# Moving half rotations and crossing halves by DMA instead of by TensorE and copies, in a three-layer fp32 transformer kernel

## The chip, the cores and the metric

The kernel runs on one core of a Trainium2 chip. The metric is the device time of one execution in microseconds; the figure quoted is the median of three runs.

## The reference

A sequence of 512 tokens with 1024 channels goes through three layers, all in float32. The first layer mixes a windowed grouped-query attention (8 query heads, 2 key heads, 64 channels each, a band of 128 tokens each way, a learned sink in the softmax) with a multi-scale pooling; the second a latent attention with a gated linear recurrence; both are followed by an MLP with squared ReLU. The third mixes a gated short convolution, a sparse attention (compressed, selected and windowed keys; for 512 tokens the last two are causal over everything) and a dilated attention (three pairs of heads with distances 1, 4 and 16), followed by an embedding gate and a norm.

What the change touches in it is the rope of the first layer's queries and keys,

```
x1, x2 = xf[..., :half], xf[..., half:]
concatenate([x1 * cos - x2 * sin, x2 * cos + x1 * sin])      # half = 32
```

and the score products `q @ k.T` of the windowed, sparse and dilated heads, with the maximum of each row that the softmax subtracts.

## The kernel before

All activations lie channel-major: a block is a tile of 128 channels by 512 tokens. Weights come from DRAM in units of 128 by 1024. For accuracy each float32 operand is cut into a high part in the matmul's fast format (`hi`, made by a copy) and a remainder (`lo`, made by a subtraction on VectorE or GpSimd), and each product is three matmuls: hi by weight hi, hi by weight lo, lo by weight hi (`mm3`). So TensorE reads weight splits `wh`, `wl`, and VectorE makes `wl` for each unit. For the later layers the splits of weights are made ahead and kept in DRAM (`keep_ahead`, tiles `kr`, `khi`, `klo`, `wk`), and fetched when needed.

**The order of the work** is written out by a planner in the program itself. `_Flow` keeps a clock `fl.now` that advances with each matmul; `_Engine` keeps a time at which VectorE, ScalarE or GpSimd would be free, from a cost formula. Main work and fill work are generators; side chains (`go`) are resumed when their due time has come. Each resumption emits instructions, so the order in which instructions stand in every engine's queue follows from that clock. `tt` gives an elementwise operation to VectorE or GpSimd and `copy` gives a copy to ScalarE or GpSimd, whichever the clock expects to finish first; an operand in PSUM keeps it off GpSimd. Transfers are all issued from SP's queue, in the order of emission, and `wl["dma"]` is the clock's guess of when the transfers issued so far are through.

**The places that the change touches.**

`rope64` (lines 1268 to 1284) turns five blocks of the first layer (one of keys, four of queries). It copies the projected block from PSUM to `zs`, multiplies `zs` on TensorE with a 128 by 128 permutation (`C("perm")`) that swaps the 32-channel halves of each head, and forms `a = zs * cos + swapped * sin` with tables `cosr`, `sinr` that hold the norm's scale; the swapped block is read from PSUM.

```
        ps2 = yield from takec("tr")
        mm(ps2, C("perm"), zs, True, True, 0.86)
        ...
        V.tensor_mul(b_, ps2, sinr)
```

`q_stacks` (956 to 965) makes two query tiles from a block z with two heads of 64 channels: for one head the upper 64 rows hold the high part of z and the lower 64 its remainder, for the other the reverse. Writing a remainder to the other half of the rows is done by the subtraction itself, one for each head. It is called for ten blocks: four of the first layer, `nq0` to `nq2`, and `dq0` to `dq2`.

`k_stacks` (967 to 978) makes for each of the block's two heads a tile `kh` with the high part of that head's 64 rows in both halves, and a tile `kl` with its remainder in both halves. That takes four copies and four subtractions of 64 rows. It is called for six blocks: one of the first layer, `ks`, `kw`, and `dk0` to `dk2`. A score is then two matmuls, `kh` by q and `kl` by q.

`Head.expo` (1004 to 1022) takes for each query block of 128 tokens the maximum of its scores from PSUM (`reduce_max`); in the windowed heads, whose scores carry a scale, it then scales it and takes the minimum with the sink (`mx`, then `nm`). ScalarE then forms the exponentials `p` with their sums. Scores of several query blocks share a PSUM bank: in the windowed heads blocks 0 and 3 (256 keys each), block 1 and block 2 (384 keys each); in the causal heads blocks 0 and 2 (128 and 384); in two dilated heads blocks 0 and 1 (128 and 256) and blocks 2 and 3 (256 each).

The first layer's attention (`attend`, jobs `job0`) starts a head's scores when its query and key stacks are there and interleaves them with fill: the remaining query blocks, the pooling and the first half of the output product.

Of the kernel before, what the change touches and what calls it, by code (L numbers as in the profile page):

```python
# [11 lines left out]
F32R = mybir.dt.float32r  # L12
# [6 lines left out]
P = 128  # L19
# [17 lines left out]
for _k, _w in _PRM:  # L37
# [3 lines left out]


_CST = (
    ("ident", 128), ("perm", 128), ("icnt", 64), ("v_cmp", 4),
    ("cos64", 512), ("sin64", 512), ("tqe", 512), ("tqo", 512), ("tk", 512),
    ("m_lo", 384), ("m_cmp", 128), ("m_d4", 512), ("m_d16", 512),
)
NKEEP = 324
_CO = {}
_n = 0  # L50
for _k, _w in _CST:
# [189 lines left out]
def _constants():  # L241
    f32 = np.float32
    cst = np.zeros((P, NCST), f32)

    def put(name, a):
        o, n = _CO[name]
        cst[:, o:o + n] = np.asarray(a, f32).reshape(P, n)

    r = np.arange(P)
    put("ident", np.eye(P))  # L250
    perm = np.zeros((P, P), f32)
    src = (r // 64) * 64 + (r % 64 + 32) % 64
    perm[src, r] = 1.0
    put("perm", perm)
    t = np.arange(T, dtype=f32)

    def rope(half):
        inv = (10000.0 ** (-(np.arange(half, dtype=f32) / f32(half)).astype(np.float64))).astype(f32)
        ang = (t[:, None] * inv[None, :]).astype(f32).astype(np.float64)
        j = r % (2 * half)  # L260
        sgn = np.where(j < half, -1.0, 1.0)
        return np.cos(ang)[:, j % half].T, np.sin(ang)[:, j % half].T * sgn[:, None]

    cs, sn = rope(32)
    put("cos64", cs)
    put("sin64", sn)
    cs, sn = rope(16)
    one = np.ones((64, T))
    put("tqe", np.concatenate([one, cs[:32], sn[:32]]))
    put("tqo", np.concatenate([cs[:32], sn[:32], one]))  # L270
    put("tk", np.concatenate([cs[:64], sn[:64]]))
    ic = np.zeros((4, 2, 8))
    for g, wd in enumerate((2, 4, 8, 16)):
        tt = np.arange(T)
        cnt = np.clip(tt + wd // 2, 0, T) - np.clip(tt - wd // 2, 0, T)
        ic[g, 0] = 1.0 / cnt[:8]
        ic[g, 1] = 1.0 / cnt[-8:]
    put("icnt", np.broadcast_to(ic.reshape(1, 64), (P, 64)))
    a, c = r[:, None], r[None, :]
    lo, up = np.where(c <= a, 0.0, NEG), np.where(c >= a, 0.0, NEG)  # L280
    put("m_lo", np.concatenate([lo, up, lo], axis=1))
    for dl in (4, 16):
        res = (a - c) % dl == 0
        full = np.where(res, 0.0, NEG)
        diag = np.where(res & (c <= a), 0.0, NEG)
        put(f"m_d{dl}", np.concatenate([full, full, full, diag], axis=1))
    tq = (np.arange(NQ)[None, :] * P + r[:, None])[:, :, None]
    n = np.arange(32)[None, None, :]
    ok = (16 * n + 31 <= tq) & (n < 31)
    put("m_cmp", np.where(ok, 0.0, NEG))  # L290
    put("v_cmp", ok.any(-1))
    return cst
# [196 lines left out]
def tile_hybrid(ctx: ExitStack, tc: tile.TileContext, wt, xT, pT, prm_d, cst_d, out):  # L489
# [24 lines left out]
    def blk(name="b", dt=F32, n=T):  # L514
        return bp.tile([P, TB], dt, tag="b", bufs=NB, name=uid(name))[:, 0:n]

    def small(n, name="s", dt=F32):
        return sp.tile([P, n], dt, tag=f"s{n}", bufs=24, name=uid(name))
# [19 lines left out]
    def takec(tag):  # L538
        while (t := bank(tag)) is None:
            yield 0.1  # L540
        return t
# [10 lines left out]
    def waitc(*tasks):  # L552
        for t in tasks:
            while not t.done:
                yield 0.1

    def f(ap):
        return ap.bitcast(F32)

    def mm(o, l, r, start, stop, us):  # L560
        PE.matmul(o, l, r, start=start, stop=stop, skip_group_check=True)  # L561
        fl.now += us
# [18 lines left out]
    def copy(out, src, scale=None):  # L581

        n, ps = width(out), src.space == PSUM
        sc = 1.0 if scale is None else scale
        e = first((S, 0.06 + n / 1090.0), *(() if ps else ((G, 0.07 + n * 0.00117 + fl.gc),)))
        if e is S:
            S.activation(out, src, AF.Copy, scale=sc)
        else:
            G.tensor_scalar(out, src, sc, 1.0, op0=ALU.mult, op1=ALU.mult)
# [185 lines left out]
    def C(name, n=None):  # L775
        o = _CO[name][0]
        n = n or _CO[name][1]
        if o + n <= NKEEP:
            return cst[:, o:o + n]
        t = blk("cst")  # L780
        nc.sync.dma_start(t[:, :n], cst_d[:, o:o + n])
        return t
# [154 lines left out]
    def v_stack(z):  # L937
# [15 lines left out]
        yield  # L953
        return lambda kb, h: r[kb // 2][0][:, kb % 2, h, :, :]

    def q_stacks(z, dst, i):

        qs = [blk("q", F32R), blk("q", F32R)]
        for r0, q in zip((0, 64), qs):
            copy(q[r0:r0 + 64], z[r0:r0 + 64])  # L960
        yield
        for r0, q in zip((0, 64), qs):
            V.tensor_sub(q[64 - r0:128 - r0], z[r0:r0 + 64], f(q[r0:r0 + 64]))
        yield
        dst[i], dst[i + 1] = qs

    def k_stacks(z, dst, i=0):

        ks = [(blk("kh", F32R), blk("kl", F32R)) for _ in range(2)]
        for r0, (kh, kl) in zip((0, 64), ks):  # L970
            copy(kh[r0:r0 + 64], z[r0:r0 + 64])
            copy(kh[64 - r0:128 - r0], z[r0:r0 + 64])
        yield
        for r0, (kh, kl) in zip((0, 64), ks):
            V.tensor_sub(kl[r0:r0 + 64], z[r0:r0 + 64], f(kh[r0:r0 + 64]))
            V.tensor_sub(kl[64 - r0:128 - r0], z[r0:r0 + 64], f(kh[r0:r0 + 64]))
        yield
        dst[i], dst[i + 1] = ks


# [11 lines left out]
    class Head:  # L992
# [11 lines left out]
        def expo(self, qbs, ps):  # L1004

            sc = self.scale
            for qb, o in qbs:
                n = self.pr[qb].shape[1]
                c = self.nm[:, qb:qb + 1]
                if sc == 1.0:  # L1010
                    V.reduce_max(c, ps[:, o:o + n], axis=AX.X, negate=True)
                else:
                    mx = small(1, "mx")
                    V.reduce_max(mx, ps[:, o:o + n], axis=AX.X)
                    V.tensor_scalar(c, mx, -sc, self.nsink, op0=ALU.mult, op1=ALU.min)
            yield
            for qb, o in qbs:
                n = self.pr[qb].shape[1]
                S.activation(self.pr[qb], ps[:, o:o + n], AF.Exp, bias=self.nm[:, qb:qb + 1], scale=sc,
                             accum_out=self.den[:, qb:qb + 1])  # L1020
            give("sc")
            yield
# [245 lines left out]
    def rope64(ps, then):  # L1268

        zs = blk("zs")  # L1270
        S.activation(zs, ps, AF.Copy)
        give("mm")
        yield
        yield from waitc(rp)
        ps2 = yield from takec("tr")
        mm(ps2, C("perm"), zs, True, True, 0.86)
        a, b_ = blk("ra"), blk("rbb")
        tt(ALU.mult, a, zs, cosr)
        yield
        V.tensor_mul(b_, ps2, sinr)  # L1280
        give("tr")
        tt(ALU.add, a, a, b_)
        yield
        yield from then(a)
# [1129 lines left out]
```

## Time and profile before

| | |
|---|---|
| median of 3 runs | 1483.72 us (1482.23 to 1487.07) |
| profiled execution | 1487.06 us, its span 1485.3 us |
| TensorE, weight loads | 1455.1 us (98%), 1179.5 us (79%) |
| VectorE, ScalarE, GpSimd | 912.5, 639.1, 327.0 us |
| granted TensorE clock | 0.989 |
| data moved by DMA | 291 MB, 196 GB/s |

PE is TensorE, PEld its weight load, DVE VectorE, ACT ScalarE, POOL GpSimd and SP SyncE, which issues the transfers. Matmuls overlap, so TensorE's busy time is the time in which at least one is under way. Most instructions of VectorE, ScalarE and GpSimd stand at line 363, most matmuls at 561 and transposes at 565, since small helpers issue them; tiles tell them apart, by names without their numbers.

### The profile page before, as it was taken

Reading aid. Unit: us, or ns where it says so; the run is one execution under the profiler, and the core shown is the slowest. Engines: PE = TensorE matmul, PEld = TensorE weight load, DVE = VectorE, ACT = ScalarE, POOL = GpSimd, SP = SyncE. Lnnn points to the kernel's source line nnn. Section 1 sums busy time; section 2 is a strip of 40 time slices with the busy share of each in tenths; the row PEclk is TensorE's granted clock in tenths of the full one; section 3 lists DMA queues with packets and bytes.
Section 4 is the critical chain, followed back from the end, with each engine's and each line's share of the span. In section 5 each row is a group of like instructions: output and inputs, shape, how many; then the busy total and the mean of one; then the engine's idle time right before and its main releaser. Section 6 shows DMA issues by size and latency. Waiting matters only on the chain.

```text
span 1485.3 us, 18855 instructions
## 1 busy us (share of the span) xinstructions
PE 1455.1 (98%) x6783; PEld 1179.5 (79%) x6786; DVE 912.5 (61%) x1419; ACT 639.1 (43%) x1174; POOL 327.0 (22%) x295
## 2 busy tenths in 40 slices
PE   9999999999999999799999999999999999999998
PEld 6778878888888887688888888888887788888787
DVE  6996864656334458987775665757755566536513
ACT  5675432323222345477342433434521575324623
POOL 4541220302102026442120220202110000111242
PEclk9999999999999999899999999999999999999999
DMA  7112688898322453332599999999855322345352
GB/s 233 43 50 79 203 275 282 262 303 283 120 91 97 146 212 143 123 132 72 173 312 318 344 322 330 333 321 331 305 206 199 113 86 108 120 171 210 116 191 93
DMA packets 117741, 291.44 MB, mean 196 GB/s; under 512 B 13072, under 2 KB 13584, under 8 KB 117648
## 3 DMA queue, kind: packets, MB, share of 16 engines
q1 hardware_dynamic: 117648, 290.25, 57.5%
q8 instruction: 53, 0.87, 0.2%
q14 instruction: 40, 0.33, 0.1%
HBM read 205.26 MB, written 84.93 MB: 195 GB/s over the span
## 4 chain that ended last, share of the span: by engine, by line
PE 84%; DVE 8%; DMA 2%; issue 2%; ACT 2%; POOL 0%; SPq 0%; POOLq 0%; DVEq 0%; ACTq 0%
PE mm L561 74%; PE sc L561 4%; PE tr L565 3%; PE av L561 3%; DVE sg L363 2%; DMA kr<-in_wt_dram 1%; PE tr L561 1%; DVE lo L363 1%; DVE mx L363 1%; DVE q L363 1%; ACT p L363 1%; DVE nm L363 0%; DVE wl L363 0%; DMA pin<-in_pT_dram 0%; DMA wr<-in_wt_dram 0%
## 5 line engine op out<-in xcount | busy, mean ns | idle before, releaser
L561 PE MATMUL mm<-hi,wh 128*128 128x512 f32 (+1 forms) x1276 | 510.5, 400 | 2.4 <-ACT hi L363 1.7
L561 PE MATMUL mm<-hi,wl 128*128 128x512 f32 (+1 forms) x1276 | 502.0, 393 | 1.4 <-DVE wl L363 1.4
L561 PE MATMUL mm<-lo,wh 128*128 128x512 f32 (+1 forms) x1276 | 501.1, 393 | 0.1
L561 PEld LDWEIGHTS mm<-lo,wh 128*128 128x128 f32 x1276 | 241.6, 189 | 56.8 <-DVE lo L363 2.1
L561 PEld LDWEIGHTS mm<-hi,wh 128*128 128x128 f32 x1276 | 242.0, 190 | 54.6 <-ACT hi L363 3.3
L561 PEld LDWEIGHTS mm<-hi,wl 128*128 128x128 f32 x1276 | 241.8, 190 | 51.5 <-DVE wl L363 2.1
L363 ACT ACTIVATE khi<-kr 128x512 fp32r<-128x512 f32 x120 | 75.9, 632 | 315.0 <-DMA kr<-in_wt_dram 305.6
L561 PE MATMUL mm<-ul,wh 128*128 128x512 f32 x512 | 202.0, 394 | 1.6 <-DVE ul L363 1.6
L561 PE MATMUL mm<-uh,wl 128*128 128x512 f32 x512 | 202.6, 396 | 0.0
L561 PE MATMUL mm<-uh,wh 128*128 128x512 f32 x512 | 202.0, 395 | 0.5 <-ACT uh L363 0.5
L363 DVE TENSOR_TENSOR wl<-wr,wh 128x1024 fp32r<-128x1024 f32 (+1 forms) x144 | 179.0, 1244 | 10.8 <-ACT wh L363 10.0
L363 DVE TENSOR_TENSOR klo<-kr,khi 128x512 fp32r<-128x512 f32 x150 | 122.5, 818 | 100.0 <-ACT khi L363 89.4
L363 ACT ACTIVATE wh<-wr 128x1024 fp32r<-128x1024 f32 (+1 forms) x142 | 146.5, 1032 | 44.3 <-PE mm L561 34.4
L363 DVE TENSOR_TENSOR x<-x,mm 128x512 f32<-128x512 f32 x112 | 76.9, 686 | 133.2 <-PE mm L561 131.3
L363 POOL TENSOR_TENSOR ma<-ma 128x512 f32<-128x512 f32 x62 | 85.4, 1378 | 275.0 <-ACT uh L363 228.4
L561 PEld LDWEIGHTS mm<-ul,wh 128*128 128x128 f32 x512 | 96.6, 189 | 24.5 <-DVE ul L363 2.1
L561 PEld LDWEIGHTS mm<-uh,wh 128*128 128x128 f32 x512 | 96.5, 189 | 23.9 <-ACT uh L363 0.9
L561 PEld LDWEIGHTS mm<-uh,wl 128*128 128x128 f32 x512 | 96.4, 188 | 22.2
L363 ACT ACTIVATE p<-sc,nm 128x512 f32<-128x512 f32 (+3 forms) x136 | 75.3, 557 | 33.9 <-DVE nm L363 25.3
L363 POOL TENSOR_SCALAR khi<-kr 128x512 fp32r<-128x512 f32 x30 | 32.2, 1075 | 254.1 <-DMA kr<-in_wt_dram 178.7
L363 DVE TENSOR_TENSOR pl<-tr,ph 128x512 fp32r<-128x512 f32 (+2 forms) x108 | 66.1, 624 | 29.9 <-ACT ph L363 29.1
L363 DVE SCALAR_TENSOR_TENSOR ma<-mm,rb 128x512 f32<-128x512 f32 x64 | 44.1, 689 | 48.6 <-PE mm L561 48.1
(291 smaller groups left out, 1642.4 us busy)
## 6 DMA issues: line engine op xcount, KB each, us to landing
wr<-in_wt_dram SPq DMA_DIRECT2D x144, 512.0 KB, 5.3
kr<-in_wt_dram SPq DMA_DIRECT2D x150, 256.0 KB, 5.9
wk<-khi SPq DMA_DIRECT2D x150, 256.0 KB, 6.0
wk<-klo SPq DMA_DIRECT2D x150, 256.0 KB, 5.7
wh<-wk SPq DMA_DIRECT2D x74, 512.0 KB, 3.3
wl<-wk SPq DMA_DIRECT2D x74, 512.0 KB, 4.2
x<-xs SPq DMA_DIRECT2D x16, 256.0 KB, 5.1
x<-in_xT_dram SPq DMA_DIRECT2D x8, 256.0 KB, 5.4
```

Of the source, the lines that this page charges most:

```text
L363: return fn(*a, **k)
L561: PE.matmul(o, l, r, start=start, stop=stop, skip_group_check=True)
L565: PE.transpose(o, i, idn)
```

## The change

The permutation goes, with its table. `rope64` copies `zs` into a tile `zw` with four transfers of 32 rows each from SBUF to SBUF, issued from SP's queue, and multiplies `zw` by `sinr` on VectorE or GpSimd. `q_stacks` copies the whole block once for one head and its lower half for the other, takes one remainder of the whole block, and moves the two remainder halves to where they belong with two transfers of 64 rows. `k_stacks` makes each head's half once, by two copies and two subtractions, and fills the other half with four transfers. After them the planner waits for a guessed landing (`moved`). `expo` takes the maxima of one bank's query blocks with one reduction where they are equally wide, and scales them together.

```
 _CST = (
-    ("ident", 128), ("perm", 128), ("icnt", 64), ("v_cmp", 4),
+    ("ident", 128), ("icnt", 64), ("v_cmp", 4),
...
-NKEEP = 324
+NKEEP = 196
...
+    def move(dst, src):
+
+        nc.sync.dma_start(f(dst), f(src))
+        wl["dma"] = max(wl["dma"], fl.now) + 0.4
+
+    def moved():
+        return max(wl["dma"], fl.now) + 2.0 - fl.now
+
+    up, dn = slice(0, 64), slice(64, 128)
+
     def q_stacks(z, dst, i):
 
-        qs = [blk("q", F32R), blk("q", F32R)]
-        for r0, q in zip((0, 64), qs):
-            copy(q[r0:r0 + 64], z[r0:r0 + 64])
-        yield
-        for r0, q in zip((0, 64), qs):
-            V.tensor_sub(q[64 - r0:128 - r0], z[r0:r0 + 64], f(q[r0:r0 + 64]))
-        yield
-        dst[i], dst[i + 1] = qs
+        qa, qb, lo = blk("q", F32R), blk("q", F32R), blk("ql", F32R)
+        copy(qa, z)
+        copy(qb[dn], z[dn])
+        yield
+        V.tensor_sub(lo, z, f(qa))
+        yield
+        move(qb[up], lo[dn])
+        move(qa[dn], lo[up])
+        yield moved()
+        dst[i], dst[i + 1] = qa, qb
 
     def k_stacks(z, dst, i=0):
 
-        ks = [(blk("kh", F32R), blk("kl", F32R)) for _ in range(2)]
-        for r0, (kh, kl) in zip((0, 64), ks):
-            copy(kh[r0:r0 + 64], z[r0:r0 + 64])
-            copy(kh[64 - r0:128 - r0], z[r0:r0 + 64])
-        yield
-        for r0, (kh, kl) in zip((0, 64), ks):
-            V.tensor_sub(kl[r0:r0 + 64], z[r0:r0 + 64], f(kh[r0:r0 + 64]))
-            V.tensor_sub(kl[64 - r0:128 - r0], z[r0:r0 + 64], f(kh[r0:r0 + 64]))
-        yield
+        (ha, la), (hb, lb) = ks = [(blk("kh", F32R), blk("kl", F32R)) for _ in range(2)]
+        copy(ha, z)
+        copy(hb[dn], z[dn])
+        yield
+        V.tensor_sub(la, z, f(ha))
+        V.tensor_sub(lb[dn], z[dn], f(hb[dn]))
+        yield
+        move(hb[up], hb[dn])
+        move(ha[dn], ha[up])
+        move(lb[up], lb[dn])
+        move(la[dn], la[up])
+        yield moved()
         dst[i], dst[i + 1] = ks
...
         def expo(self, qbs, ps):
 
             sc = self.scale
-            for qb, o in qbs:
+            ns = [self.pr[qb].shape[1] for qb, _ in qbs]
+
+            sets = [qbs] if len(set(ns)) == 1 else [[q] for q in qbs]
+            for g in sets:
+                (qb, o), m = g[0], len(g)
                 n = self.pr[qb].shape[1]
-                c = self.nm[:, qb:qb + 1]
+                c = self.nm[:, qb:g[-1][0] + 1:max(1, g[-1][0] - qb)]
+                p3 = ps[:, o:o + m * n].rearrange("p (a n) -> p a n", n=n)
                 if sc == 1.0:
-                    V.reduce_max(c, ps[:, o:o + n], axis=AX.X, negate=True)
+                    V.reduce_max(c, p3, axis=AX.X, negate=True)
                 else:
-                    mx = small(1, "mx")
-                    V.reduce_max(mx, ps[:, o:o + n], axis=AX.X)
+                    mx = small(2, "mx")[:, :m]
+                    V.reduce_max(mx, p3, axis=AX.X)
                     V.tensor_scalar(c, mx, -sc, self.nsink, op0=ALU.mult, op1=ALU.min)
...
+        zw = blk("zw")
+        for r in range(0, P, 32):
+            move(zw[r:r + 32], zs[(r ^ 32):(r ^ 32) + 32])
+        t = fl.now + moved()
         yield from waitc(rp)
-        ps2 = yield from takec("tr")
-        mm(ps2, C("perm"), zs, True, True, 0.86)
         a, b_ = blk("ra"), blk("rbb")
         tt(ALU.mult, a, zs, cosr)
-        yield
-        V.tensor_mul(b_, ps2, sinr)
-        give("tr")
+        yield max(0.0, t - fl.now)
+        tt(ALU.mult, b_, zw, sinr)
         tt(ALU.add, a, a, b_)
```

## Rows read from the trace of the kernel before

**Rows 1.** The page: TensorE's busy time, and the chain that ended last by engine.

```profile
PE 1455.1 (98%) x6783; PEld 1179.5 (79%) x6786; DVE 912.5 (61%) x1419; ACT 639.1 (43%) x1174; POOL 327.0 (22%) x295
...
PE 84%; DVE 8%; DMA 2%; issue 2%; ACT 2%; POOL 0%; SPq 0%; POOLq 0%; DVEq 0%; ACTq 0%
```

**Rows 2.** Busy us of each engine (instructions) in single stretches, granted clock, DMA share, GB/s.

```profile
20.00:60.00 40.00, 40.00 (x181) 30.74 (x180) 33.07 (x44) 14.83 (x29) 26.37 (x20) 1.00 0.30 87
60.00:110.00 50.00, 44.73 (x244) 35.80 (x243) 47.24 (x111) 40.83 (x105) 19.17 (x19) 0.97 0.13 40
...
200.00:220.00 20.00, 17.90 (x70) 13.84 (x69) 12.02 (x15) 6.92 (x10) 4.56 (x4) 0.91 0.86 292
...
570.00:640.00 70.00, 59.64 (x251) 47.93 (x250) 62.62 (x86) 31.53 (x57) 40.54 (x31) 0.88 0.32 114
...
1100.00:1370.00 270.00, 270.00 (x1412) 218.32 (x1414) 150.22 (x315) 113.66 (x287) 24.12 (x32) 0.99 0.41 148
```

**Rows 3.** Waits of TensorE, 55 to 130 us: total, times, longest.

```profile
PE tr L565 <- ACT p L363: 2.4, 3, 1.4
PE mm L561 <- DVE wl L363: 1.4, 2, 0.8
```

**Rows 4.** Timeline of TensorE around the fourth rotation: start us, us, instruction.

```profile
44.93 0.39 PE L561 MATMUL mm<-lo,wh 128*128 128x512 f32 x1
...
45.16 1.02 PE L561 MATMUL tr<-zs,cst 128*128 128x512 f32 x2
...
45.61 0.79 PE L561 MATMUL mm<-hi,wh 128*128 128x512 f32 x1
...
46.25 0.40 PE L561 MATMUL mm<-hi,wl 128*128 128x512 f32 x1
...
46.71 0.40 PE L561 MATMUL sc<-kh,q 128*128 128x256 f32 x2
```

**Rows 5.** VectorE's groups by form, 20 to 130 us: busy us, mean ns, idle before.

```profile
L363 DVE TENSOR_TENSOR q<-ra,q 64x512 fp32r<-64x512 f32 x8 | 9.5, 1192 | 0.3
...
L363 DVE TENSOR_SCALAR nm<-mx,nsink 128x1 f32<-128x1 f32 x32 | 6.8, 214 | 1.1
...
L363 DVE TENSOR_REDUCE mx<-sc 128x1 f32<-128x256 f32 x16 | 6.6, 414 | 0.0
...
L363 DVE TENSOR_TENSOR kl<-ra,kh 64x512 fp32r<-64x512 f32 x4 | 4.4, 1112 | 0.0
...
L363 DVE TENSOR_TENSOR rbb<-tr,cst 128x512 f32<-128x512 f32 x5 | 3.4, 685 | 0.7 <-PE tr L561 0.7
```

**Rows 6.** Timeline of VectorE: a maximum over 512 columns.

```profile
1343.73 0.69 DVE L363 TENSOR_REDUCE nm<-sc 128x1 f32<-128x512 f32 x1 [1.39 <-PE sc L561]
```

**Rows 7.** Timeline of GpSimd and VectorE at 51 us.

```profile
51.10 2.14 POOL L363 TENSOR_TENSOR ra<-ra,rbb 128x512 f32<-128x512 f32 x1 [3.89 <-DVE rbb L363]
52.01 1.78 DVE L363 TENSOR_TENSOR ra<-zs,cst 128x512 f32<-128x512 f32 x1
```

**Rows 8.** The page's DMA issues: count, KB each, median us to landing.

```profile
wk<-khi SPq DMA_DIRECT2D x150, 256.0 KB, 6.0
...
xs<-x SPq DMA_DIRECT2D x8, 256.0 KB, 2.1
```

**Rows 9.** Timeline: the last remainders of two key stacks, and a score.

```profile
38.77 4.49 DVE L363 TENSOR_TENSOR kl<-ra,kh 64x512 fp32r<-64x512 f32 x4
...
1350.51 2.81 DVE L363 TENSOR_TENSOR kl<-z,kh 64x512 fp32r<-64x512 f32 x4 [0.76 <-ACT kh L363]
...
1356.44 0.40 PE L561 MATMUL sc<-kh,q 128*128 128x512 f32 x1
```

**Rows 10.** Waits in SP's queue, 15 to 130 us: total, times, longest.

```profile
SPq L622 <- DVE wl L363: 55.5, 8, 15.9
SPq L622 <- POOL wl L363: 47.3, 5, 21.9
```

**Rows 11.** Timeline of ScalarE at 206 us: idle before it, and what ended it.

```profile
206.74 0.63 ACT L363 ACTIVATE khi<-kr 128x512 fp32r<-128x512 f32 x1 [4.60 <-DMA kr<-in_wt_dram]
```

More of the change, by code (lines that the diff above doesn't have):

```diff
@@ L250, in _constants @@
     put("ident", np.eye(P))
[L251 to L254, printed above, removed]
     t = np.arange(T, dtype=f32)
```

## The prediction

> **What bounds the kernel now.** I read the page's busy table first, then its chain of work that ended last, then busy times of eleven stretches, then the waits of single ones. TensorE is busy 98% of the span and carries 84% of the chain [rows 1]. So a microsecond of matrix work removed is a microsecond won, unless the other engines can't follow. The stretches say where they can't. From 20 to 60 us TensorE is busy all 40 us. In the first attention, 60 to 110, it is busy 44.73 of 50 us while VectorE is busy 47.24: 5.3 us of idle time, and the granted clock of 0.97, partly the lower level of 1.2 GHz, costs 50 x 0.03 = 1.5 us more [rows 2]. Its waits there name the exponentials, which wait for maxima taken on VectorE, and weight remainders made on VectorE [rows 3]. In 200 to 220, at the start of the first MLP, are 2.1 us of idle time and 20 x 0.09 = 1.8 us of lost clock; in 570 to 640, behind the recurrent block, 10.4 us idle. From 1100 to 1370 TensorE is never idle [rows 2].
>
> The change touches three places: the rope and stacks at 20 to 60 us with the attention behind them, the stacks of the sparse attention (from 1105), and those of the dilated attention (to 1356).
>
> **The permutation matmuls.** Each rope loses one fp32 matmul, which runs as two passes. Around the fourth, the first pass starts at 45.16, one ordinary matmul follows at 45.61, the next at 46.25 [rows 4]. From 45.16 to 46.25 are 1.09 us for two passes and one ordinary matmul; the pitch of ordinary ones is 0.23 (44.93 to 45.16), so a rotation costs 0.86 us. Five go: -4.3 us of TensorE time, in a stretch in which it is never idle.
>
> **VectorE in the first attention.** If VectorE didn't get shorter too, the 4.3 us would come back as idle time after 60 us. What leaves it: a query pair needed two subtractions and needs one; four pairs at 1.192 us, 4.8 us. A key stack needed four and needs two; one stack at 1.112, 2.2 us. Of a head's blocks 0 and 3 (both 256 wide), two reductions of 0.414 and two scalings of 0.214 become one reduction of 512 columns, 0.69 [rows 5, 6], and one scaling: 2 x 0.414 + 2 x 0.214 - 0.69 - 0.214 = 0.35 us, for eight heads 2.8 us. Together 9.8 us, twice what TensorE gives up. ScalarE and GpSimd lose two half copies of the keys; the number of query copies stays, one of each pair now full height at the same columns. Not all 9.8 us count: the planner gives weight remainders and products to whichever of VectorE and GpSimd it thinks free first, so work now on GpSimd moves onto VectorE. I credit two of the 6.8 us of stalls and lost clock, -2.0 us, with bounds of 0 (refilled) and -6.8 (all gone); late next would be ScalarE's exponentials, 40.83 us of ScalarE in these 50 [rows 2].
>
> The later stacks save 6 + 10 subtractions too (six query pairs, five key stacks), 16 x 0.70 = 11 us by the four that end a key stack in 2.81 us [rows 9], but their cover is matrix work without a gap from 1100 to 1370 [rows 2]: nothing; with that cover gone they would be worth up to those 11 us. The merged maxima of two dilated heads, 0.1 us each by the reductions alone, are hidden by the same.
>
> A row speaks against the credit. The product with the sines read one operand from PSUM and took 0.685 us [rows 5]; now it reads both from SBUF. A product of that form, the one with the cosines, took 1.78 us when GpSimd's addition, from 51.10 for 2.14 us, ran over it [rows 7]. Five such delays of 1.1 us are 5.5 us: the relief would fall from 9.8 to 4.3 us, just TensorE's saving, and the sum to -4.3 + 1.0 = -3.3 us. I don't take this for all five, but it is one way into the second rival. The Trainium skill's page "SBUF — State Buffer", section "Who interferes with whom", states the rule: a VectorE instruction with two SBUF inputs and a GpSimd instruction that reads SBUF exclude one another, and one with a single SBUF input doesn't contend. The pair of rows agrees with it.
>
> **What is added: 64 transfers on SP's queue** (four for each of five ropes, two for each of ten query pairs, four for each of six key stacks), 64 or 128 KB each. The trace of before has no copy from SBUF to SBUF. The nearest are stores of SBUF, 256 KB in 2.1 us, and in the burst of kept weights 6.0 us [rows 8]. So 2.1 to 6.0 us each; I take the low end for 20 to 60 us, where the DMA share is 0.30, and 4 us after 1100, where it is 0.41 [rows 2]. By the Trainium skill's page "DMA: Bandwidth & Descriptors", section "Anatomy of one DMA — SWDGE (gpsimd) path", a copy costs about 2.0 us plus its bytes at 436 GB/s, an estimated 2.3 us here, by which the sum would stay what it is; no row of before shows this kind of copy.
>
> The planner reckons 0.4 us for each move and 2.0 us behind them, and issues scores only after that; other matmuls go first. What counts is the excess over the plan, less the time by which TensorE comes later than planned. In the dilated attention the last key remainder ended at 1350.51 + 2.81 = 1353.3 and its score began at 1356.44: 3.1 us of slack, which covers an excess of 4 - 2.4 = 1.6 us. In the first attention the key remainders ended at 38.77 + 4.49 = 43.3 and the first score began at 46.71, 3.4 us later [rows 4, 9]. Two remainders fewer end 2.2 us earlier, four moves with 4 x 0.4 us of issue and 2.1 of flight put 3.7 us behind them: 1.9 us of slack, while the score itself may come up to 3.4 us earlier for want of four rotations. I put one stall of +1.0 us there; bounds 0 and +5 (the flight at 6.0).
>
> The new waits stand in the queue of VectorE or GpSimd (the sine product, for the rotated halves), and behind it there queue maxima and weight remainders; and in TensorE's (a score, for a stack), and behind it stands everything. SP's queue keeps its weight loads in order, moves between them; 64 issues at 0.4 us are 26 us of its time, spread over the kernel, and the loads run several units ahead: nothing.
>
> **Sum.** -4.3 - 2.0 + 1.0 = -5.3 us. The profiled execution took 1487.06 us (span 1485.3 and 1.8 around it), 0.2% above the median of 1483.72; less 5.3 it is 1481.8, and the median becomes 1478.4. About 0.3%, 4.45 us, is what a measurement of this kernel can tell from no change.
>
> **Rivals.**
> 1. *The forecast*, 1478.4, own range 1474.5 to 1481.5. Chance 0.50.
> 2. *The gain is eaten by the new order.* The planner writes every engine's order from its own clock, so five shorter ropes shift all later decisions; VectorE is refilled, or sine products are slowed as above. No relief and a stall of 3 us: -4.3 + 3 = -1.3, 1482.4 (1480.4 by the sine products alone). For it: the 3.9 us lost at 200 to 220 come with such an order (ScalarE's copy of a kept weight waits 4.60 us for its transfer, the square for the MLP behind it [rows 11]) and can come up elsewhere. Against: 1100 to 1370, where the same kinds of waits cost nothing. Chance 0.25.
> 3. *The vector side was the whole bottleneck.* All 6.8 us go, -4.3 - 6.8 = -11.1: 1472.6; if the hole at 200 to 220 closes too (3.9), 1468.7. For it: 9.8 us against 6.8. Against: ScalarE, busy 40.83 of the 50 us, keeps all its exponentials [rows 2]. Chance 0.12.
> 4. *Slower: the moves stand behind blocked loads.* SP issues in order, and from 15 to 130 us its weight loads wait 55.5 us for remainders on VectorE and 47.3 on GpSimd, the longest 15.9 and 21.9 us [rows 10]. The key stack's moves behind one such wait hold up the first score. Of 15.9 us the slack of 3.4 is hidden, 12.5 are not: -4.3 - 2.0 + 12.5 = +6.2, 1489.9. It decides (over +4.45) from new stalls of 10.8 us. For it: these waits are longer than the slack. Against: such a load waits for a remainder queued before the move, which is mostly done by then. Chance 0.13.
>
> That the change does nothing can be excluded for the rotations: the instructions are gone.
>
> **Chances and range.** Faster: three quarters of the forecast (0.38) and rival 3 (0.12), 0.50. Slower: rival 4, 0.13. The same: the rest, 0.37. The range from 1470.5 to 1486.0 leaves out the far part of rival 3 (0.04) and rival 4.
>
> **What would show it.** The fp32 passes gone, and the work up to 60 us ending some 4 us earlier; idle time in the first attention below 5.3 us with VectorE less busy; moves landing in 2 to 4 us before 60; no wait of TensorE on a stack over 2 us. Wrong if a score or a sine product waits long for a move, if moves stand behind a waiting load, or if the idle time at 60 to 110 grows by what the rotations freed.

## The result

The changed kernel takes 1497.17 us (median of 4 runs, 1493.77 to 1502.03), the kernel before beside it 1482.97: ratio 1.0088, 95% interval 1.0069 to 1.0107. It is slower by some 13 us (the medians differ by 14.2); forecast were 1478.4 us, and a chance of 0.13 that it is slower.

The page of the changed kernel, busy times and chain, against [rows 1]:

```profile
PE 1458.9 (97%) x6776; PEld 1182.1 (79%) x6776; DVE 897.9 (60%) x1382; ACT 634.1 (42%) x1169; POOL 312.9 (21%) x285
...
PE 83%; DVE 7%; DMA 5%; issue 2%; ACT 2%; POOL 1%; SPq 1%; DVEq 0%; POOLq 0%; ACTq 0%
```

VectorE's busy time fell by 14.6 us, as meant, and GpSimd's by 14.1, of which 6.0 are 30 copies of kept weights (`khi`) that merely took less time each. TensorE's busy time rose by 3.8 us without the five rotations: its granted clock is 0.986 in place of 0.989, and the three largest groups of matmuls, of the same number, took 4.4 us more by the two pages. Transfers went from 2% of the chain to 5%. The stretches, in the columns of [rows 2]:

```profile
20.00:60.00 40.00, 34.95 (x150) 28.01 (x149) 25.06 (x30) 11.54 (x21) 22.80 (x17) 0.92 0.55 145
60.00:110.00 50.00, 43.39 (x223) 34.05 (x221) 41.91 (x90) 35.03 (x93) 17.93 (x21) 0.94 0.14 43
...
1100.00:1370.00 270.00, 269.76 (x1408) 218.21 (x1406) 134.97 (x278) 102.76 (x256) 22.82 (x28) 0.99 0.47 162
1390.00:1400.00 10.00, 6.33 (x37) 5.01 (x35) 5.89 (x25) 4.20 (x15) 0.00 (x0) 0.94 0.44 158
1400.00:1410.00 10.00, 9.28 (x42) 7.19 (x42) 4.24 (x7) 8.64 (x19) 3.05 (x3) 0.72 0.01 2
```

From 20 to 60 us, where TensorE never paused before [rows 2], it is idle for 5.05 us and loses 40 x 0.08 = 3.2 us of clock. From 60 to 110 it is idle for 6.61 (before 5.27) and loses 50 x 0.06 = 3.0 (before 1.5). That is 11.1 us more than before in these 90 us, against 4.3 saved; another 2.2 (1.18 idle, 1.0 of clock) follow from 110 to 160, where before had none. A second hole stands at 1390 to 1410, where the work after the dilated scores runs out: 4.39 us idle and 3.4 of clock. Before had a smaller one there, 2.86 us idle at 1370 to 1390, at the full clock.

Two marks divide the span: the first matmul of the first MLP, at 203.4 us before and 213.7 after (+10.3); and the way from the copy of the compressed keys (`kch`, 1157.9 and 1168.2) to the end, 327.4 us before and 332.0 after (+4.6). Between the marks nothing is lost (954.5 us in both). The profiled executions were the longest of their kernels, after's 4.9 us above its median and before's 4.1.

How far one trace can be trusted is shown by another kernel with the same instructions up to 1290 us (e7, below). Its granted clock from 0 to 20 us is 0.91 where after's is 1.00, which is 20 x 0.09 = 1.8 us that no edit made; still its first mark stands at 211.8, and between the marks it needs 950.6 us. Over all the traces below that middle takes 947.4 to 954.5 us, and the clock of the first 20 us is 1.00 in before, after, e2, e4, e6, e8, e10, e13 and e14 and 0.91 in the other nine. So the marks of two traces can be compared only to within some 2 to 4 us, and marks do not add up to medians. With e7's slow start counted, +7 to +10 belong to the first attention.

SP's queue around the first attention (start, us, instruction; wr is a weight load, the rest are the moves):

```profile
34.64 0.33 SPq L618 DMA_DIRECT2D wr<-in_wt_dram  x1
35.08 2.40 SPq L954 DMA_DIRECT2D zw<-zs  x4
46.61 0.33 SPq L618 DMA_DIRECT2D wr<-in_wt_dram  x1
47.04 1.15 SPq L954 DMA_DIRECT2D kh<-kh  x2
48.24 1.23 SPq L954 DMA_DIRECT2D kl<-kl  x2
49.52 1.24 SPq L954 DMA_DIRECT2D q<-ql  x2
50.85 2.69 SPq L954 DMA_DIRECT2D zw<-zs  x4
```

VectorE in the same time, and TensorE's first score:

```profile
40.41 2.72 DVE L359 TENSOR_TENSOR kl<-ra,kh 128x512 fp32r<-128x512 f32 x2
43.16 1.68 DVE L359 TENSOR_TENSOR ql<-ra,q 128x512 fp32r<-128x512 f32 x1
...
45.37 1.21 DVE L359 TENSOR_TENSOR wl<-wr,wh 128x1024 fp32r<-128x1024 f32 x1
...
55.12 0.69 DVE L359 TENSOR_TENSOR rbb<-zw,cst 128x512 f32<-128x512 f32 x1 [6.01 <-DMA zw<-zs]
```

```profile
54.53 0.76 PE L557 MATMUL sc<-kh,q 128*128 128x256 f32 x2 [3.70 <-DMA q<-ql]
```

The key remainders are done at 40.41 + 2.72 = 43.13 us, the query's at 44.84. Their moves wait until 46.61: ahead of them in SP's queue stands a load of a weight unit whose buffer is read by the remainder `wl` that VectorE ends at 45.37 + 1.21 = 46.58. Then ten moves go out one behind another, each 0.6 us of SP's time. The first score, which waited for nothing at 46.71 before [rows 4], comes at 54.53, and VectorE, whose next instruction is a sine product, idles for 6.01 us. SP's waits from 15 to 130 us against [rows 10], and the moves of the whole run (count, KB, median us from issue to landing):

```profile
SPq L618 <- DVE wl L359: 83.2, 12, 22.7
SPq L618 <- POOL wl L359: 6.3, 2, 4.1
```

```profile
q<-ql SPq DMA_DIRECT2D x20, 128.0 KB, 3.2
...
kh<-kh SPq DMA_DIRECT2D x12, 128.0 KB, 5.5
kl<-kl SPq DMA_DIRECT2D x12, 128.0 KB, 5.2
...
zw<-zs SPq DMA_DIRECT2D x20, 64.0 KB, 4.0
```

At the dilated end the loads of the embedding's input stand late in the queue (before they were issued at 1372.17; with the 10.3 us of the first mark that would be 1382.5), and TensorE has nothing else to do when it waits for them (two rows, SP and TensorE):

```profile
1393.93 0.90 SPq L2264 DMA_DIRECT2D pin<-in_pT_dram  x2
```

```profile
1400.60 0.80 PE L557 MATMUL mm<-hi,wh 128*128 128x512 f32 x1 [2.71 <-ACT hi L359]
```

### The profile page after: what moved, and what is told of

Read it like the earlier page. It is cut to its first block, busy times and chain, and to the rows that moved or that the text cites. A ratio compares the mean times of both kernels' runs of the same rounds, so it can differ in the third digit from the quotient of the medians.

```text
span 1500.2 us, 18935 instructions
## 1 busy us (share of the span) xinstructions
PE 1458.9 (97%) x6776; PEld 1182.1 (79%) x6776; DVE 897.9 (60%) x1382; ACT 634.1 (42%) x1169; POOL 312.9 (21%) x285
## 4 chain that ended last, share of the span: by engine, by line
PE 83%; DVE 7%; DMA 5%; issue 2%; ACT 2%; POOL 1%; SPq 1%; DVEq 0%; POOLq 0%; ACTq 0%
PE mm L557 71%; PE sc L557 4%; PE av L557 3%; PE tr L561 3%; DMA kr<-in_wt_dram 3%; DVE sg L359 2%; PE tr L557 1%; DVE wl L359 1%; DVE lo L359 1%; DMA kl<-kl 0%; DVE klo L359 0%; DMA pin<-in_pT_dram 0%; DVE kz L359 0%; SPq L954 0%; DMA x<-in_xT_dram 0%
## 5 line engine op out<-in xcount | busy, mean ns | idle before, releaser
L359 DVE TENSOR_TENSOR wl<-wr,wh 128x1024 fp32r<-128x1024 f32 (+1 forms) x147 | 182.7, 1244 | 11.2 <-ACT wh L359 10.4
L359 POOL TENSOR_SCALAR khi<-kr 128x512 fp32r<-128x512 f32 x30 | 26.2, 873 | 251.1 <-DMA kr<-in_wt_dram 225.3
```

The lines of the kernel that those rows point to most:

```text
L359: return fn(*a, **k)
```

## The experiments

The theory after this reading: two places cost the time, the moves behind a blocked load with a landing longer than the planner reckons, and the late pin load. Its rivals: the transfers cost by themselves; the sine product, now with both operands in SBUF, slows VectorE and GpSimd; and the order alone, shifted as a whole, costs that much with no transfer at fault. "Mark" is the start of the first MLP, "end part" the time from `kch` to the end of the span, both of the profiled execution; ratios are to the kernel before.

| run | median us | ratio (95%) | mark | end part |
|---|---|---|---|---|
| before | 1483.9 | | 203.4 | 327.4 |
| after | 1497.17 | 1.0088 (1.0069 to 1.0107) | 213.7 | 332.0 |
| e1 maxima alone | 1485.44 | 1.0004 (0.9994 to 1.0014) | 205.9 | 326.5 |
| e2 rotations alone | 1492.39 | 1.0047 (1.0032 to 1.0062) | 216.3 | 327.1 |
| e3 stacks alone | 1490.33 | 1.0039 (1.0027 to 1.0051) | 207.4 | 328.9 |
| e4 after, moves on ScalarE's queue | 1495.79 | 1.0073 (1.0056 to 1.0090) | 210.7 | 332.6 |
| e5 e2, sine product on VectorE | 1488.68 | 1.0032 (1.0022 to 1.0042) | 211.4 | 326.5 |
| e6 after, loads held back | 1490.65 | 1.0045 (1.0030 to 1.0060) | 207.2 | 330.3 |
| e7 after, pin load early | 1488.57 | 1.0027 (1.0016 to 1.0038) | 211.8 | 324.0 |
| e8 after, guess 6 us | 1487.21 | 1.0021 (1.0010 to 1.0031) | 206.2 | 329.0 |
| e9 before, retimed | 1489.37 | 1.0034 (1.0022 to 1.0046) | 210.9 | 326.5 |
| e10 after, guess, pin, sine | 1482.44 | 0.9988 (0.9977 to 0.9999) | 207.0 | 324.0 |
| e11 after, held, pin, sine | 1482.37 | 0.9988 (0.9978 to 0.9997) | 207.6 | 323.5 |
| e12 maxima + early pin | 1481.24 | 0.9983 (0.9974 to 0.9992) | 206.1 | 322.1 |
| e13 e12, rotation left out | 1480.84 | 0.9979 (0.9969 to 0.9989) | 206.1 | 324.1 |
| e14 e12 + rotations by transfer | 1485.80 | 1.0010 (0.9999 to 1.0022) | 210.1 | 321.9 |
| e15 e12 + stacks by transfer | 1485.37 | 1.0012 (1.0001 to 1.0024) | 208.4 | 324.4 |
| e16 e12, retimed | 1478.62 | 0.9969 (0.9957 to 0.9982) | 205.8 | 321.8 |

**The parts, each alone in the kernel before** (e1 to e3: `expo`; `rope64`; `q_stacks` and `k_stacks` taken over from the changed kernel).

> The kernel before with the merged maxima alone. Queue theory (the key stack's moves stand in SP's queue behind a weight load that waits for a remainder on VectorE, the first score waits, and TensorE falls to 1.2 GHz): no moves here, so 0 to 3 us faster than before, from 8 x 0.35 us of VectorE time in the first attention. Flight theory (the moves simply take longer than the planner reckons, in whatever queue): the same. Re-timing theory (any edit that shifts the planner's clock reorders the queues and meets other holes, so the loss has little to do with moves): anything from 6 faster to 6 slower, with the change at places that the edit does not touch.

> The kernel before with the rotations by transfers alone; stacks and maxima as before. Queue theory: the sine products of the last ropes wait for moves behind loads, but no score waits for a move directly: between 4 us faster (the rotations' own time) and 4 slower. Flight theory: 64 KB moves of 2 to 5.5 us against 3.6 reckoned, 0 to 5 us slower. Re-timing theory: 6 faster to 6 slower, with the change outside 20 to 130 us.

> The kernel before with the stacks' crossing halves by transfers alone. In its queue order the key stack's moves and the first query pair's follow one another with no weight load issued between the copies and them. Queue theory: the first attention loses 0 to 4 us against before, not 10; the dilated attention may lose up to 6. Flight theory: the first score still waits some 4 us and TensorE still falls to 1.2 GHz, 8 to 14 us slower in all, most of it before 130 us. Re-timing theory: no forecast for the place, 6 faster to 6 slower.

0.04 + 0.47 + 0.39 = 0.90%: the parts add up to the whole, 0.88%. The merged maxima bring nothing. Rotations and stacks each cost by themselves here (e9 tells how much the order alone can do, and with the longer guess, in e10, e14 and e15, the parts do not add). e2, 7 to 8 us slower, lies outside the ranges of all three theories, which none had above 6. In e3 no load stood ahead of the first moves, and no first score waited, as the queue theory said; its mark is 4.0 us later than before. In e2 the score waits for VectorE, not for a move (VectorE, GpSimd, TensorE of e2):

```profile
40.45 8.46 DVE L359 TENSOR_TENSOR kl<-ra,kh 64x512 fp32r<-64x512 f32 x4
48.94 3.33 DVE L359 TENSOR_TENSOR q<-ra,q 64x512 fp32r<-64x512 f32 x2
```

```profile
42.02 1.30 POOL L359 TENSOR_TENSOR rbb<-zw,cst 128x512 f32<-128x512 f32 x1
43.39 1.62 POOL L359 TENSOR_TENSOR ra<-ra,rbb 128x512 f32<-128x512 f32 x1
44.98 1.71 POOL L359 TENSOR_TENSOR ra<-zs,cst 128x512 f32<-128x512 f32 x1
46.66 1.71 POOL L359 TENSOR_TENSOR rbb<-zw,cst 128x512 f32<-128x512 f32 x1
```

```profile
50.73 0.77 PE L557 MATMUL sc<-kh,q 128*128 128x256 f32 x2 [5.63 <-DVE q L359]
```

Four key remainders take 8.46 us under GpSimd's back-to-back products; before they took 4.49 [rows 9].

**The sine product on VectorE** (e5, on top of e2):

```
-        tt(ALU.mult, b_, zw, sinr)
+        V.tensor_mul(b_, zw, sinr)
```

> The rotations by transfers alone, as in e2, but the sine product stays on VectorE. In e2 the first score waited 5.6 us for a query remainder: four key remainders took 8.5 us of VectorE while GpSimd ran sine products and additions over them. Contention theory (the product that left PSUM went to GpSimd, and GpSimd's products slow VectorE's): the four remainders take under 5 us, the first score waits under 2 us, the first MLP begins 4 us or more earlier than in e2 (216.3), and the whole is 3 to 9 us faster than e2. Move theory (the transfers' wait is what delays the ropes): the first score still waits 4 us or more and the whole stays within 2 us of e2.

The same four remainders of e5:

```profile
40.25 4.25 DVE L359 TENSOR_TENSOR kl<-ra,kh 64x512 fp32r<-64x512 f32 x4
```

The contention is real, 4.2 us at this place, the first score waits no more, and the run is 3.7 us shorter, all as the contention theory said. But TensorE now waits 4.75 us at 49.87 for a weight remainder that the planner gave to GpSimd instead, and 0.32 of e2's 0.47% stay.

**The moves' queue** (e4: `nc.scalar.dma_start` for `nc.sync.dma_start` in `move`, the order kept).

> The changed kernel with the same order of every engine's work; only the 64 moves are issued from ScalarE's queue in place of SP's. Queue theory: the moves no longer stand behind the waiting load; the first score waits under 1 us, and the first MLP begins at most 3 us later than before in place of 10. Against it ScalarE itself issues 64 moves, at 0.5 us each 32 us over the whole run, and waits in order for the remainders. Flight theory: the first score still waits 3 us or more, and the first MLP still begins 7 us or more late. Re-timing theory: the order is the changed kernel's, so the loss stays within 3 us of its 14.

The first score comes at 50.4 us instead of 54.53 and waits for no move. But TensorE's waits for ScalarE's high parts, from 15 to 130 us, grow from 1.1 to 3.5 us, since a move that waits in ScalarE's queue holds up ScalarE's own copies, and 8.3 of the 50 us from 60 to 110 are idle (after: 6.61). The mark is 3.0 us earlier than after, which is within what two traces of the same instructions differ by, and the median 1.4 us, within the noise. Of the three forecasts only the re-timing theory's holds whole: with the order kept, the loss stays within 3 us of what it was, although the first score waits for no move. Another queue isn't free of a jam, and freeing the first score alone isn't shown to bring anything.

**Loads held back** (e6, no weight load is issued between the first key stack's or query pair's start and its moves; the guess of 2.0 us stays) **and a longer guess** (e8).

```
     def moved():
-        return max(wl["dma"], fl.now) + 2.0 - fl.now
+        return max(wl["dma"], fl.now) + 6.0 - fl.now
```

> The changed kernel, but no weight load is issued between the start of the first key stack or the first query pair and its moves, so the load that stood before them comes after. Queue theory: the key stack's moves go out 4 us or more earlier, the first score waits under 1.5 us (3.7 before), and the first MLP begins 3 to 8 us earlier than in the changed kernel (213.7). Flight theory (the moves' own issue and flight are too long): the first score still waits 2.5 us or more, and the first MLP begins less than 2 us earlier. In both the dilated attention is as in the changed kernel.

> The changed kernel, with the planner reckoning 6.0 us behind a move in place of 2.0, so that it puts other work before scores and sine products. Flight theory (the guess was too short for moves of 2 to 7 us): no wait on a move over 0.5 us is left in TensorE, and it is 4 to 10 us faster than the changed kernel. Queue and contention theories: the moves still stand behind loads and GpSimd still slows VectorE; the waits shift to other places, and the whole stays within 4 us of the changed kernel; the dilated attention gets no shorter, since its scores come later still.

Both free the first score of its wait for a move and bring the mark from 213.7 to 207.2 and 206.2. e6 does what the queue theory said, e8 what the flight theory said, and the landings tell why both can: the key stack's moves, 15 to 75 us, of after and then of e6 (count, KB, median us to landing).

```profile
kh<-kh SPq DMA_DIRECT2D x2, 128.0 KB, 5.2
kl<-kl SPq DMA_DIRECT2D x2, 128.0 KB, 4.9
```

```profile
kh<-kh SPq DMA_DIRECT2D x2, 128.0 KB, 2.2
kl<-kl SPq DMA_DIRECT2D x2, 128.0 KB, 2.3
```

In after a load of 512 KB was issued just ahead of them; with it held back they land in 2.2 us, and in e4, on the other queue, in 2.2 and 2.3. In e8, where the load is ahead again, they take 5.1 and 4.6. So the long flight at this place comes with the load, not with the move. The first score of e8 still comes as late as after's 54.53, but TensorE does other work until then:

```profile
54.50 0.40 PE L557 MATMUL sc<-kh,q 128*128 128x256 f32 x2
```

The first two stretches of e8:

```profile
20.00:60.00 40.00, 39.12 (x185) 31.69 (x183) 31.73 (x39) 13.95 (x24) 25.82 (x21) 1.00 0.56 152
60.00:110.00 50.00, 43.39 (x223) 34.73 (x224) 41.50 (x85) 36.38 (x95) 28.34 (x28) 0.93 0.20 60
```

TensorE has work from 20 to 60 again, at the full 2.4 GHz. The loads still block SP in e8; what the longer guess changes is that nothing is lined up behind the moves meanwhile. e6 is less clean: its idle time from 20 to 110 us, 2.25 + 9.59 = 11.8, is no less than after's 11.7, since other waits come up (3.92 us for a remainder of the exponentials, at 94.93). What it loses less is clock, 1.5 us in these 90 against 6.2.

**The pin load early** (e7: the two loads of the embedding's input at the start of the third layer's last phase, their splits 8 us later).

```
+    def pin_load():
+        for c in range(2):
+            t = blk("pin")
+            nc.sync.dma_start(t, pT[:, c, :])
+            go(pin_split(pl[c], t))
...
+    pin_load()
     jobs = []
```

> The changed kernel with the two loads of the embedding input (tiles pin) issued at the start of the dilated attention and cut 8 us later, in place of when the embedding products begin. Tail theory (the later scores push these loads to where TensorE has nothing else, so it waits for them and falls to 1.2 GHz): from the first compressed key to the last output block of the dilated attention (yd) 243 us or less in place of 248.6, and 4 to 7 us faster than the changed kernel. Stack theory (the dilated scores wait for their own moves): that stretch stays above 246 us. Before 1160 us nothing changes in either.

The hole is gone (e7, the columns of [rows 2]), and the median is 8.6 us lower, more than the 4 to 7 that the tail theory said:

```profile
1390.00:1400.00 10.00, 10.00 (x64) 8.86 (x63) 4.91 (x8) 9.83 (x20) 0.00 (x0) 1.00 0.30 109
1400.00:1410.00 10.00, 9.86 (x50) 8.05 (x49) 6.18 (x9) 6.15 (x12) 5.67 (x4) 1.00 0.27 98
```

The end part falls by 8.0 us, more than the 4.6 that the change had added. e12 says why: the same edit without any transfer takes 4.4 us off the end part of e1 (326.5 to 322.1). So, by one trace each, 8.0 - 4.4 = 3.6 us of the loss was the pin load made later; the rest was to be had in the kernel before too.

**All mended, and the order alone** (e9: one number in the kernel before).

```
-        mm(ps2, C("perm"), zs, True, True, 0.86)
+        mm(ps2, C("perm"), zs, True, True, 0.46)
```

> The kernel before with one number of the planner changed: it reckons 0.46 us for each permutation matmul instead of 0.86. Every instruction is kept; only the order in which the planner writes them can shift. If the loss comes from the named places (moves behind a waiting load, their flight, the late pin load), a mere shift costs or gains under 3 us: 1480 to 1486. If any shift of the planner's clock costs as much as the change did (the second rival, the order itself), it ends 5 us or more above before: 1488 or more.

> The changed kernel with three edits together: the planner's guess of a move's landing 6.0 us instead of 2.0, the pin load early, the sine product on VectorE. If the three causes stand side by side and add, it is the 1487.2 of the guess alone, less the 4.2 us that its dilated stretch still lost (246.8 against 242.6), less 0 to 2.5 for the sine product: 1480.5 to 1483, the kernel before again and no faster. If the rotations' 4.3 us come out once the stacks are waited for properly: 1476 to 1479. If the edits only shift the order: 1485 to 1490.

> The changed kernel with the weight loads held back while the first key and query stacks are made (the guess of 2.0 us stays), the pin load early, the sine product on VectorE. If the causes add: 1490.65 less 6 us for the pin load, less 0 to 3.7 for the sine product: 1481 to 1485. If holding back the loads costs what the moves gain: 1486 to 1490.

> The kernel before with the merged maxima and the pin load early; no half goes by DMA. If the early pin load only takes away the wait that the changed kernel had, nothing is to be won here: 1483 to 1486. If an early pin load is worth something by itself (TensorE's two short waits at the dilated end go): 1480 to 1482.

e10 and e11 are back at the kernel before, where adding up the causes had put them, and not below e12, which has none of their transfers. e9 missed what the theory said of it: with no instruction changed it is 0.34% slower, its mark 7.5 us later, 1.8 of them by its slower first 20 us; its longest wait in the first attention is 3.82 us for VectorE. A theory in which only the named places cost time doesn't hold.

**Where the freed time goes** (e13 to e16; in e13 the `perm` matmul goes and the product reads `zs`; e14 and e15 take `rope64`, or the stacks, from the changed kernel with the guess of 6 us; e16 is e9's edit on e12).

> The kernel before with merged maxima and early pin load (1481.24 us by itself), and the rotation left out: the sine product reads the block itself instead of its swapped halves, so neither a permutation matmul nor a transfer is made. It shows the most that taking the five permutations off TensorE can bring. If TensorE sets the end there, as the prediction's first step has it: 4.3 us less, 1476 to 1478. If the first attention is bound by the vector side and the 4.3 us come back as idle time: 1480 to 1482.5. If the shifted order costs more than it saves, as the retimed kernel before did: 1484 or more.

> Rotations by transfers (guess 6.0 us, sine product on VectorE), merged maxima, early pin load; stacks by copies as before. If rotations by transfers, properly waited for, bring what they free: 1476 to 1478. If they bring nothing: 1480 to 1483. If they cost by themselves, as the two kernels with rotations alone did (5 to 7 us): 1485 to 1488.

> Stacks by transfers (guess 6.0 us), merged maxima, early pin load; rotations by TensorE as before. If the stacks' moves, waited for, cost only the 1.4 to 1.9 us by which the end from the dilated keys on is longer with them: 1482 to 1484. If the spared VectorE time pays: 1478 to 1480. If they cost as they did alone (5.8 us): 1486 to 1488.

> A second shift of the order alone: merged maxima, early pin load, and the planner's cost of a permutation matmul 0.46 us instead of 0.86. Same instructions as the 1481.24 us kernel. If the 5 us of the first retimed kernel belong to that planner cost: 1485 to 1487. If such a shift throws the time by some us in either direction without a rule: anywhere from 1478 to 1487, so that differences of this size between two orders are no evidence on the operations.

The same two stretches of e12, then of e13, and the longest wait of e13 before 60 us (TensorE, and the GpSimd instruction that it waits for):

```profile
20.00:60.00 40.00, 39.26 (x178) 30.38 (x178) 34.68 (x43) 15.33 (x29) 24.41 (x19) 1.00 0.27 87
60.00:110.00 50.00, 42.96 (x242) 33.98 (x240) 46.44 (x96) 42.05 (x107) 20.22 (x20) 1.00 0.13 40
```

```profile
20.00:60.00 40.00, 35.85 (x153) 28.65 (x154) 33.84 (x39) 13.88 (x25) 25.50 (x18) 0.91 0.29 87
60.00:110.00 50.00, 43.69 (x246) 35.16 (x245) 43.90 (x91) 39.91 (x102) 21.43 (x26) 1.00 0.12 38
```

```profile
48.65 0.80 PE L557 MATMUL mm<-hi,wl 128*128 128x512 f32 x1 [3.26 <-POOL wl L359]
45.94 2.65 POOL L359 TENSOR_TENSOR wl<-wr,wh 128x1024 fp32r<-128x1024 f32 x1
```

With the rotation simply left out, TensorE idles 4.15 us from 20 to 60 instead of 0.74 and loses 40 x 0.09 = 3.6 us of clock; the mark stands at 206.1 in both, though e13 has the faster first 20 us, and the medians are 0.4 us apart. Most of the idle time is one wait for a weight remainder on GpSimd. In e12 GpSimd began the remainder at this place at 43.49 and TensorE never waited for it; in e13 a copy of a key, one of a weight and one of a query come first. So e13 doesn't isolate the rotations: its order shifts too, and its sine product reads both operands from SBUF.

e14 and e15 are 4.6 and 4.1 us slower than e12. But e10, which has both kinds of transfer, the same guess and the same early pin load, is only 1.2 slower than e12: the two don't add, so these 4 us are not simply the price of the transfers; the order is likely part of them. e16, by the edit that cost e9 0.34%, is the fastest kernel of the study, 0.31% under before and 2.6 us under e12, though the two intervals overlap. At least the edit doesn't cost 5 us again: what one planner number does in one kernel, it needn't do in the next.

## Why the prediction was wrong

Two steps of the sum failed. The -4.3 us of the rotations did not come out. And the stall, put at +1.0 us, with the moves' time in SP's queue put at nothing, was 3.70 us at the first score alone; with the waits and the lost clock around it, 11.1 us more than before went from 20 to 110 us. Of the prediction's own signs of being wrong two are there in full, the score's wait for a move and the moves behind a waiting load; of the third, idle time from 60 to 110 us, 1.3 of 4.3 us.

- **"-4.3 us of TensorE time, in a stretch in which it is never idle".** The step that failed first. The instructions went, but a stretch without idle time is no proof that TensorE sets its end: when TensorE needs less, what the other engines make can come too late. In e13, without any transfer, that is a weight remainder on GpSimd (3.26 us at 48.65), and the gain is 0.4 us, within the scatter. Whether another order would let the 4.3 us out stays open, since the order alone is worth as much.
- **The slack of 3.4 us at the first score.** It was reckoned from the key remainders (43.3). The score also needs the query stack, and VectorE makes that behind them; its first remainder in the kernel before:

```profile
43.29 2.78 DVE L363 TENSOR_TENSOR q<-ra,q 64x512 fp32r<-64x512 f32 x1
```

  It ended at 43.29 + 2.78 = 46.07, and the score that reads it began at 46.71: 0.64 us of slack, not 3.4. Nor did the key remainders end 2.2 us earlier for being two fewer: 43.13 after, 43.26 before.
- **The stall of +1.0 us.** Forecast were 0.4 us of issue and 2.1 of flight a move. Measured were 0.6 us, and 5.2 and 4.9 for the key stack's flight, behind a blocked queue: a wait of 3.70 at a score that came 7.8 us later, waits for weight remainders and lost clock besides. The 2.1 was right for a move with no load just ahead (2.2 in e6). That the score is late isn't itself the cost, since e8's is as late; that TensorE stood at it is.
- **Rival 4, "the moves stand behind blocked loads" (0.13).** This is what happened, by the very wait it names ([rows 10]; SP blocked on `wl` until 46.61), and the reason given against it was wrong: the load's remainder was queued behind the stacks' remainders (45.37 against 40.41), not ahead. It was priced at 1489.9, with 12.5 us of the longest wait falling on the score; the real wait held SP for 9.0 us and the finished key remainders for 3.5 (43.13 to 46.61), and the loss is larger because other places added to it. e6 and e8, which take the score's wait away, are 6.5 and 10.0 us faster than after.
- **The VectorE credit of -2.0.** TensorE's idle time from 60 to 110 rose instead, though VectorE is busy 41.91 us there, not 47.24. The relief is real, but just ahead, at 55.12, VectorE had stood 6.01 us for rotated halves, and 2.6 of TensorE's 6.61 us of idle time are waits for weight remainders that VectorE makes. That the one brought the other is argued, not shown.
- **The sine product, weighed and set aside.** The rule of the Trainium skill's page "SBUF — State Buffer", section "Who interferes with whom", that spoke against the change holds here: key remainders of 1.06 us each by e5 (4.25 for four) became 2.1 (8.46) under GpSimd's products. Where rotations stand alone, e2 against e5, the two differ by 3.7 us, a shift of the order included.
- **The late stacks and the 64 issues, costed at nothing.** TensorE stayed busy to 1370 (269.76 of 270). But the end part is about 2 us longer with moved stacks even with an early pin load (e7, e10, e11, e15: 323.5 to 324.4; e12, e14, e16, with copied ones: 321.8 to 322.1; e13, with copied ones too, is an exception at 324.1, so the 2 us are likely and not shown), and the pin load that the moves push back costs 3.6. That loss had no place in the sum.
- **Rival 2, the order.** Priced at up to 3 us, it is as large as anything else: 5.4 us up in e9, 2.6 down in e16. So of the 7 to 10 us at the first mark, some 3 to 7 go with the moves' waits: two different edits (e6, e8) take these away and agree in it, though each shifts the order too, and e4, which keeps the order, gains little. All of these lie inside what orders without a single transfer show (marks of 203.4 to 210.9). That the moves waited and TensorE stood is shown; how much of the whole loss is theirs and how much the order's stays open.

## What to carry to other kernels

A transfer that replaces an engine's work stands in somebody's queue: before it is costed, look which blocked instruction stands ahead of it there, and whose queue it blocks in turn. What counts is not when the waiting instruction comes but whether the engine has other work until then (e8). TensorE busy without a gap, where a planner fills the gaps, doesn't tell that TensorE sets the end; leaving the work out altogether (e13) costs one run, and its trace names the next wait. And where the order is computed, retime it without changing an instruction first: a forecast smaller than what that does (here up to 5.4 us) can't be told from the order.

## What the runs showed of the hardware

- Moves from SBUF to SBUF of 64 to 128 KB took 2.1 us (the fastest of a rotation's) to 7.1 us (the slowest of a key's high part) in the changed kernel. The first attention's key moves took 2.2 and 2.3 with no load just ahead of them in their queue (e6, e4) and 4.6 to 5.2 with one (after, e8). The 2.3 estimated in the prediction by the Trainium skill's page "DMA: Bandwidth & Descriptors" agrees with the former; for the latter the measurement decides. Some moves are slower than the stores of 256 KB in 2.6 us of the same profile.
- Issuing a move took SP about 0.6 us (2.40 for four, 1.15 to 1.24 for two), a weight load 0.33 to 0.54.
- A subtraction of 64 x 512 with both operands in SBUF took 0.70 us late in the kernel with GpSimd idle beside it [rows 9], 1.06 in e5 beside some of its copies, and 2.1 in e2 beside its products without a break.
- Idle time can cost about as much again in clock, or nothing: e13 is idle 4.15 us from 20 to 60 us, and the granted clock of 0.91 there takes 3.6 more; e12 is idle 7.04 us from 60 to 110, in waits of at most 1.8 us, and keeps 1.00. The same instructions can have it either way: from 40 to 60 us after idles 5.05 us at 0.85 and e7 4.72 us at 1.00.
